# Weaving GLA blocks over the retention's projections, one pipe for both, and w_out gated page by page into DRAM

## The chip, the cores and the metric

The kernel runs on one core of one Trainium2 chip. The metric is the device time of one execution in microseconds: the median of the runs. TensorE multiplies matrices, VectorE and GpSimd work elementwise, ScalarE evaluates functions and copies, SyncE (SP) issues most DMAs. "PSUM" is TensorE's output memory, "SBUF" the memory beside it.

## The reference

Two transformer blocks follow each other on x of 1024 x 1024 (float32). The change concerns the first block's token mixer:

```python
proj = u @ w_in                                   # rq rk rv rg gq gk gv gg glr
ro = head_norm(retention(rope(rq), rope(rk), rv), center=True) * silu(rg)
log_a = log_sigmoid(glr @ gla_gate_w + gla_gate_b) / 16
go = head_norm(gla(gq / 8, gk, gv, log_a), center=False) * silu(gg)
m = concat([ro, go]) @ w_out
x = layer_norm(ALPHA * x + gate1 * m)
```

Retention and gated linear attention (GLA) have four heads each and carry a state from one stretch of the sequence to the next. `gate1` is a vector over the 1024 output columns, so `gate1 * (y @ w_out)` is `y @ (w_out * gate1)`: the kernel multiplies it into w_out's columns. The feed-forward layer, and the whole second block, follow.

## The kernel before

Every large product is made exact to about float32 by splitting each operand into a high and a low part (`split`, L82 the copy on ScalarE, L83 the subtraction on VectorE) and running three matmuls for each 128 rows of the contraction (`mm3`, L114 to L116). One output tile of 128 x 512 over a contraction of 1024 is a *group* of 24 matmuls. Weights come in pages of 128 x 1024: loaded into a page of tag S (six buffers) by SP, then split into two pages of tag W or X (eight buffers each). Pages of tag H (eight buffers) hold the blocks' data.

The order of the first mixer is written in `build` with Python generators. `gla_proj` computes GLA's projections and stores them in DRAM (g_qkb, gv, gg). Then `ret_proj` runs 24 groups, yielding after each: eight for the retention's gate (`tok_proj`, stored as rg through SP) and sixteen for its q and k (stored as r_qk through ScalarE's queue). `weave(main, side, n)` takes n steps of the side generator for each step of the main one and then runs what is left of the side.

The side is `pipe` over eight `gla_block`s of 128 tokens. One step of `pipe` starts a new block and advances each live one by a stage, the newest first. A GLA block has three stages:

- Stage 0: loads gv, gg and g_qkb (L520, L521, L523). For each of two pairs of heads, GpSimd makes seven differences (L531), ScalarE takes the absolute value and the exponential (L533, L534), VectorE multiplies q in (L536) and GpSimd k (L537). TensorE computes the scores (L544) into PSUM of tag "sc", of which there are two buffers. VectorE evicts each with a product (L549) or masked copies (L552), four evictions a buffer.
- Stage 1: decayed q and k (L560 to L564), the output matmuls (L567, L569), a transpose (L573), the state's update (L578, L583) and the statistics of the head norm (L454 and on).
- Stage 2: the gate on GpSimd (L475), transposes (L478), the scaling on ScalarE (L446), the store to g_od (L588).

The weave is 0.3: a pipe step after each 3.33 groups. When the groups are done, the rest of the GLA pipe runs. Then `ret_setup` loads tables and the weight of v (`r_W`, in W pages). `gate1` is broadcast over the partitions into a page of tag "bc" (three buffers, L73), and `wout_load` takes w_out's rows of k = 4 to 7 (four pages: load L668, gating on GpSimd L672, split into X pages). Then the pipe over eight `ret_block`s: loads of r_qk (L623 to L625), k_rot (L626) and rg (L628), the value group, the rotation (L631 on GpSimd, L632 and L633 on VectorE), scores (L637), transposes (L642), output and state (L648 to L654), head norm, store to r_od (L657). `block1_out` loads and gates the other half of w_out, into W pages that the value weight leaves, and multiplies.

The code's order is not each engine's order. The framework plans, when the program is built, the order of every engine's and every queue's instructions, with the code's order as priority and its own estimates of the durations; on the chip each engine then keeps that order and waits where something is not ready. In the trace the first gating operations of w_out stand among the GLA blocks, and the broadcast of gate1 was issued at 310.51 us, long before the code's place for it.

```python
run(n.weave(n.ret_proj(T), n.pipe(n.gla_block(i) for i in range(NB)), 0.3))
n.ret_setup()
n.gate1 = n.bcast(n.mod["gate1"][0])
n.wout = n.wout_load(I["w_out"], n.gate1, (4, 6))
run(n.pipe(n.ret_block(i, T) for i in range(NB)))
```

Of the kernel before, what the change touches and what calls it, by code (L numbers as in the profile page):

```python
# [10 lines left out]
ALU = mybir.AluOpType  # L11
# [3 lines left out]
S = 1024  # L15
D = 1024
FF = 4096
NB = 8
# [6 lines left out]
class Net:  # L25
# [21 lines left out]

    BUFS = dict(U=4, X=8, H=8, W=8, S=6, half=6, ev=4, bc=3)

# [34 lines left out]

    def wpage(self, src, r0, c0, C, kt=None, gate=None, tag="W"):
        kt = kt or 1024 // C
        st = self.page("S")
        hi = self.page(tag, F32R)
        lo = self.page(tag, F32R)
        sv = st[:, 0:kt * C]  # L90
        self.nc.sync.dma_start(
            out=sv.rearrange("p (k c) -> p k c", c=C),
            in_=src[r0:r0 + 128 * kt, c0:c0 + C].rearrange("(k p) c -> p k c", p=128))
        if gate is not None:
            self.nc.gpsimd.tensor_tensor(out=sv, in0=sv, in1=gate, op=ALU.mult)
        self.split(sv, hi[:, 0:kt * C], lo[:, 0:kt * C], self.w_eng)
        return (hi[:, 0:kt * C].rearrange("p (k c) -> p k c", c=C),
                lo[:, 0:kt * C].rearrange("p (k c) -> p k c", c=C))

    def wcols(self, src, c0, C, K=1024, tags="W"):  # L100

        per = min(1024 // C, K // 128)
        out = []
        for k in range(0, K // 128, per):
            h, l = self.wpage(src, 128 * k, c0, C, per, tag=tags[k * len(tags) // (K // 128)])
            out += [(h[:, j, :], l[:, j, :]) for j in range(per)]
        return out
# [257 lines left out]
def _rows(ap, t):  # L365
    return ap[t * 128:(t + 1) * 128, :]


class Mix1(Net):


    def feat_out(self, T, W, m, h, ps_tag="mm"):

        ps = self.ps(ps_tag)
        self.mm3(ps, [(a[:, m], b[:, m]) for a, b in W], self.act_rhs(T, h))
        return ps

    def tok_out(self, T, W, t, C=512, ps_tag="mm"):
        ps = self.ps(ps_tag)
        self.mm3(ps[:, 0:C], self.act_lhs(T, t), W)  # L380
        return ps
# [98 lines left out]

    def pipe(self, gens, oldest=False):

        live, gens, d = [], list(gens), 1 if oldest else -1
        while gens or live:
            if gens:
                live.append(gens.pop(0))
            live = [g for g in live[::d] if next(g, self) is not self][::d]
            yield

# [166 lines left out]
        yield from self.head_norm(o[:, 0], vg[:, 512:1024], self.norm_w[:, 0:4], True, A, kT)  # L656
        nc.sync.dma_start(out=self.r_od[:, :, sl], in_=kT)  # L657

    def wout_load(self, src, gate=None, ks=(0, 2, 4, 6), out=None):

        nc = self.nc
        out = out or [[None] * 8 for _ in range(2)]
        for n in range(2):
            for k in ks:
                st = self.page("S")
                tag = "W" if k < 4 else "X"
                hi, lo = self.page(tag, F32R), self.page(tag, F32R)
                nc.sync.dma_start(out=st.rearrange("p (k c) -> p k c", c=512),  # L668
                                  in_=src[128 * k:128 * k + 256, 512 * n:512 * n + 512].rearrange("(k p) c -> p k c", p=128))
                if gate is not None:  # L670
                    sv = st.rearrange("p (k c) -> p k c", c=512)
                    nc.gpsimd.tensor_tensor(out=sv, in0=sv, op=ALU.mult, in1=gate[:, 512 * n:512 * n + 512].unsqueeze(1)  # L672
                                            .broadcast_to([128, 2, 512]))
                self.split(st, hi, lo)
                for j in range(2):
                    out[n][k + j] = (hi[:, j * 512:j * 512 + 512], lo[:, j * 512:j * 512 + 512])
        return out
# [25 lines left out]
    def block1_out(self):  # L703

        nc, I = self.nc, self.I
        T = self.new_T()
        lw, lb = self.bcast(I["ln1_w"][0]), self.bcast(I["ln1_b"][0])
        self.x1d = self.dram([S, D], "x1")

        def finish(i, y):  # L710
            self.normalize(y, y, True)
            nc.vector.tensor_tensor(out=y, in0=y, in1=lw, op=ALU.mult)
            nc.vector.tensor_tensor(out=y, in0=y, in1=lb, op=ALU.add)
            nc.sync.dma_start(out=_rows(self.x1d, i), in_=y)
            self.normalize(y, y, True)
            self.to_T(y, i, T, self.mod["scale2"], self.mod["shift2"])

        W = self.wout_load(I["w_out"], self.gate1, (0, 2), self.wout)
        yield from self.out_stage(W, [(self.r_od, 4), (self.g_od, 4)], I["x"], finish)
        return T  # L720

# [1107 lines left out]
def build(tc, I, out):  # L1829
    from contextlib import ExitStack  # L1830
    with ExitStack() as ctx:
        n = Mix2(tc, ctx, I, out)
        n.modulation()
        n.kv_mem()
        def run(g):
            while True:
                try:
                    next(g)
                except StopIteration as e:
                    return e.value  # L1840

        def delay(g, k):
            for _ in range(k):
                yield
            yield from g

        norm, kv = n.first_norm(I["x"]), n.kv_proj()
        T, steps = None, [3, 0, 1, 0, 1]
        while T is None:
            n.w_eng = n.nc.gpsimd  # L1850
            for _ in range(steps.pop(0) if steps else 1):
                next(kv, None)
            n.w_eng = n.nc.vector
            T = next(norm)
        run(kv)
        def early():
            for _ in range(3):
                yield
            yield from n.mods()
            yield from n.s5_setup()  # L1860
        run(n.weave(n.gla_proj(T), early(), 0.75))
        n.gla_setup()
        run(n.weave(n.ret_proj(T), n.pipe(n.gla_block(i) for i in range(NB)), 0.3))
        n.ret_setup()
        n.gate1 = n.bcast(n.mod["gate1"][0])
        n.wout = n.wout_load(I["w_out"], n.gate1, (4, 6))
        run(n.pipe(n.ret_block(i, T) for i in range(NB)))
        T = run(n.block1_out())
        T = n.block1_mlp(T)
        n.dt_proj(T)  # L1870
        xbc = n.xbc_proj(T)
        for g, side in ((n.s5_mixer(T), (3, 1)), (n.rg_mixer(T), (1, 3))):
            for _ in g:
                for _ in range(side[0] if side else 0):
                    next(xbc, None)
                side = side[1:]
        run(xbc)
        n.ssd_setup()
        n.wout = n.wout_load(I["w_out_2"])
        out = n.block2_out()  # L1880
        T = next(out)
        run(n.weave(n.pipe(n.ssd_block(i) for i in range(NB)), delay(out, 3)))
        T = run(n.attention(T))
        n.block2_mlp(T)
# [86 lines left out]
```

## Time and profile before

| what | value |
|---|---|
| median of 3 runs | 2657.97 us (2657.94 to 2659.93) |
| the profiled execution | 2657.86 us |
| its span | 2655.9 us |
| mean granted clock of TensorE | 0.979 |
| TensorE busy | 2541.6 us, 96% |
| VectorE, ScalarE, GpSimd busy | 1879.1, 1172.0, 239.3 us |

The span is the time between the first and the last instruction of the program in the profiled execution. A clock of 1.00 is full speed, 0.50 the lower of the two levels. In rows of the timeline a bracket gives the idle time of the engine before the instruction and what ended it; "SPq" is a DMA issue on SP's queue. Times within the trace are microseconds from the span's start.

### The profile page before, as it was taken

What the parts mean: (1) busy time and instruction counts of PE and PEld (TensorE: products, weight loads), DVE (VectorE), ACT (ScalarE), POOL (GpSimd) and SP (SyncE); (2) the same over time, 40 slices, a digit from 0 to 9 for tenths busy, and PEclk for the clock granted to TensorE, in tenths of its full rate; (3) what the DMA queues carried; (4) which work ended last, traced back from release to release, by engine and by line L of the source; (5) the groups of instructions that cost most, each with busy time, mean ns of one, the idle gap of its engine ahead of it and who ended that gap; (6) DMA issues with size and microseconds to landing.
All of it is one profiled execution on the core that took longest, in us unless ns stands there. A gap on an engine that the chain in (4) does not pass through costs nothing. (4 is left out here: it accounts for less than half of the span.)

```text
span 2655.9 us, 33016 instructions
## 1 busy us (share of the span) xinstructions
PE 2541.6 (96%) x12086; PEld 2065.0 (78%) x12086; DVE 1879.1 (71%) x3205; ACT 1172.0 (44%) x1866; POOL 239.3 (9%) x222
## 2 busy tenths in 40 slices
PE   7899999889999999999999998999998999999997
PEld 6586777677888888888877776778876888888886
DVE  4858666678897777646865567785568777767786
ACT  3622233344654444433643474552237454444342
POOL 4121135540000000000000003100000000000000
PEclk8899999999999999999999999999998999999999
DMA  9772433464266569866632243361102755799783
GB/s 334 253 256 100 146 100 99 140 168 149 78 230 222 195 231 328 305 192 229 199 149 64 82 143 115 116 222 56 40 32 88 256 191 210 245 341 337 263 284 106
DMA packets 255130, 484.36 MB, mean 182 GB/s; under 512 B 21604, under 2 KB 110964, under 8 KB 254968
## 3 DMA queue, kind: packets, MB, share of 16 engines
q1 hardware_dynamic: 247768, 470.59, 52.2%
q10 hardware_dynamic: 7200, 11.67, 1.2%
q8 instruction: 95, 1.56, 0.3%
q14 instruction: 67, 0.55, 0.1%
HBM read 338.80 MB, written 143.38 MB: 182 GB/s over the span
## 5 line engine op out<-in xcount | busy, mean ns | idle before, releaser
L114 PE MATMUL ps<-U,W 128*128 128x512 f32 (+1 forms) x1080 | 427.3, 396 | 10.4 <-ACT ev L776 5.1
L115 PE MATMUL ps<-U,W 128*128 128x512 f32 (+1 forms) x1080 | 425.6, 394 | 1.5 <-DVE U L341 1.5
L114 PE MATMUL ps<-W,H 128*128 128x512 f32 x1088 | 424.4, 390 | 0.4 <-DVE X L1069 0.3
L116 PE MATMUL ps<-U,W 128*128 128x512 f32 (+1 forms) x1080 | 423.5, 392 | 0.8 <-DVE W L83 0.8
L83 DVE TENSOR_TENSOR W<-S,W 128x1024 fp32r<-128x1024 f32 (+1 forms) x272 | 333.1, 1228 | 128.5 <-ACT W L82 127.5
L115 PE MATMUL ps<-W,H 128*128 128x512 f32 x1088 | 423.9, 390 | 0.0
L116 PE MATMUL ps<-W,H 128*128 128x512 f32 x1088 | 423.9, 390 | 0.0
L82 ACT CAST W<-S 128x1024 fp32r<-128x1024 f32 x288 | 298.6, 1043 | 242.2 <-PE ps L115 161.1
L82 ACT CAST H<-S 128x1024 fp32r<-128x1024 f32 x130 | 136.6, 1050 | 287.4 <-PE ps L115 200.7
L83 DVE TENSOR_TENSOR H<-S,H 128x1024 fp32r<-128x1024 f32 x130 | 158.6, 1220 | 146.0 <-ACT H L82 141.2
L114 PEld LDWEIGHTS ps<-U,W 128*128 128x128 f32 (+1 forms) x1080 | 201.2, 186 | 60.9 <-ACT ev L776 5.4
L115 PEld LDWEIGHTS ps<-U,W 128*128 128x128 f32 (+1 forms) x1080 | 201.2, 186 | 49.5 <-DVE U L341 4.6
L114 PEld LDWEIGHTS ps<-W,H 128*128 128x128 f32 x1088 | 204.3, 188 | 43.4 <-DVE X L1069 1.2
L116 PEld LDWEIGHTS ps<-U,W 128*128 128x128 f32 (+1 forms) x1080 | 201.2, 186 | 46.8 <-DVE W L83 1.9
L116 PEld LDWEIGHTS ps<-W,H 128*128 128x128 f32 x1088 | 204.3, 188 | 41.9
L115 PEld LDWEIGHTS ps<-W,H 128*128 128x128 f32 x1088 | 204.3, 188 | 41.7
L116 PE MATMUL ps<-W,U 128*128 128x512 f32 x352 | 139.8, 397 | 5.5 <-DVE U L83 5.5
L114 PE MATMUL ps<-W,U 128*128 128x512 f32 x352 | 141.8, 403 | 2.6 <-DVE X L274 2.0
L115 PE MATMUL ps<-W,U 128*128 128x512 f32 x352 | 140.3, 398 | 0.0
L776 ACT ACTIVATE ev<-ev 128x512 f32<-128x512 f32 x104 | 65.5, 630 | 152.4 <-DVE ev L874 122.5
L116 PEld LDWEIGHTS ps<-W,U 128*128 128x128 f32 x352 | 67.0, 190 | 20.7 <-DVE U L83 6.8
L777 ACT ACTIVATE X<-ev 128x512 f32<-128x512 f32 x128 | 81.0, 634 | 3.5
(529 smaller groups left out, 4505.1 us busy)
## 6 DMA issues: line engine op xcount, KB each, us to landing
S<-mlp_h SPq DMA_DIRECT2D x112, 512.0 KB, 5.1
S<-in_w_ff SPq DMA_DIRECT2D x96, 512.0 KB, 5.1
mlp_h<-X SPq DMA_DIRECT2D x96, 512.0 KB, 4.2
S<-in_mlp_w SPq DMA_DIRECT2D x96, 512.0 KB, 4.9
mlp_w<-S SPq DMA_DIRECT2D x96, 256.0 KB, 2.5
S<-mlp_w SPq DMA_DIRECT2D x48, 512.0 KB, 4.8
S<-in_w_in SPq DMA_DIRECT2D x46, 512.0 KB, 5.3
X<-in_w_ada SPq DMA_DIRECT2D x32, 512.0 KB, 6.8
```

What stands on the lines that cost most here:

```text
L82: self.nc.scalar.copy(out=hi, in_=src)
L83: (lo_eng or self.nc.vector).tensor_tensor(out=lo, in0=src, in1=hi.bitcast(F32), op=ALU.subtract)
L114: mm(out=ps, lhsT=lh, rhs=rh, start=start and k == 0, stop=False)
L115: mm(out=ps, lhsT=lh, rhs=rl, start=False, stop=False)
L116: mm(out=ps, lhsT=ll, rhs=rh, start=False, stop=stop and k == n - 1)
L776: nc.scalar.activation(out=r, in_=x, func=ACTF.Relu)
L777: nc.scalar.activation(out=out, in_=r, func=ACTF.Square)
```

## The change

- `pipe` takes its blocks from an iterator that it asks once a step, so that the iterator can do work of its own between blocks.
- The weave is 0.42 instead of 0.3.
- `blocks()` yields the eight GLA blocks; behind each it takes one step of `gated`. Then it runs what is left of the projections, sets the retention up, yields an empty generator, and yields the eight retention blocks, with `wout_load` of k = 4 to 7 in front of the second.
- `gated` loads a page of w_out, multiplies it by gate1 on GpSimd and stores it in a DRAM tensor, one page a step, eight in all. gate1's broadcast is emitted before the projections.
- `wout_load` has no gating left; its two calls for the first mixer read the gated tensor.

```diff
     def pipe(self, gens, oldest=False):
-        live, gens, d = [], list(gens), 1 if oldest else -1
-        while gens or live:
-            if gens:
-                live.append(gens.pop(0))
+        live, gens, d = [], iter(gens), 1 if oldest else -1
+        while True:
+            g = next(gens, None)
+            if g is not None:
+                live.append(g)
+            elif not live:
+                return
             live = [g for g in live[::d] if next(g, self) is not self][::d]
             yield
...
+    def gated(self, src, gate):
+        nc = self.nc
+        d = self.dram([D, D], "gated")
+        for k in (4, 6, 0, 2):
+            for n in range(2):
+                st = self.page("S").rearrange("p (k c) -> p k c", c=512)
+                io = lambda w: w[128 * k:128 * k + 256, 512 * n:512 * n + 512].rearrange("(k p) c -> p k c", p=128)
+                nc.sync.dma_start(out=st, in_=io(src))
+                nc.gpsimd.tensor_tensor(out=st, in0=st, op=ALU.mult, in1=gate[:, 512 * n:512 * n + 512].unsqueeze(1)
+                                        .broadcast_to([128, 2, 512]))
+                nc.sync.dma_start(out=io(d), in_=st)
+                yield d
...
-    def wout_load(self, src, gate=None, ks=(0, 2, 4, 6), out=None):
+    def wout_load(self, src, ks=(0, 2, 4, 6), out=None):
...
-                if gate is not None:
-                    sv = st.rearrange("p (k c) -> p k c", c=512)
-                    nc.gpsimd.tensor_tensor(out=sv, in0=sv, op=ALU.mult, in1=gate[:, 512 * n:512 * n + 512].unsqueeze(1)
-                                            .broadcast_to([128, 2, 512]))
                 self.split(st, hi, lo)
...
-        W = self.wout_load(I["w_out"], self.gate1, (0, 2), self.wout)
+        W = self.wout_load(self.wg, (0, 2), self.wout)
...
-        run(n.weave(n.ret_proj(T), n.pipe(n.gla_block(i) for i in range(NB)), 0.3))
-        n.ret_setup()
-        n.gate1 = n.bcast(n.mod["gate1"][0])
-        n.wout = n.wout_load(I["w_out"], n.gate1, (4, 6))
-        run(n.pipe(n.ret_block(i, T) for i in range(NB)))
+        gated = n.gated(I["w_out"], n.bcast(n.mod["gate1"][0]))
+        proj = n.ret_proj(T)
+
+        def blocks():
+            for i in range(NB):
+                yield n.gla_block(i)
+                n.wg = next(gated)
+            run(proj)
+            n.ret_setup()
+            yield iter(())
+            for i in range(NB):
+                if i == 1:
+                    n.wout = n.wout_load(n.wg, (4, 6))
+                yield n.ret_block(i, T)
+
+        run(n.weave(proj, n.pipe(blocks()), 0.42))
```

## Rows read from the trace of the kernel before

**Rows 1.** The page: its first line and TensorE's busy time.
```profile
span 2655.9 us, 33016 instructions
...
PE 2541.6 (96%) x12086; PEld 2065.0 (78%) x12086; DVE 1879.1 (71%) x3205; ACT 1172.0 (44%) x1866; POOL 239.3 (9%) x222
```

**Rows 2.** Busy time by stage: stretch, length, engines, granted clock, DMA share, GB/s.
```profile
280.00:301.57 21.57, 21.57 (x96) 17.57 (x95) 16.77 (x49) 2.77 (x5) 0.00 (x0) 1.00 0.33 123
301.57:477.07 175.50, 159.13 (x965) 131.10 (x964) 102.26 (x244) 58.30 (x108) 76.01 (x108) 0.96 0.33 110
477.07:525.92 48.85, 37.06 (x257) 29.25 (x257) 39.27 (x110) 18.10 (x43) 26.36 (x13) 0.93 0.50 149
525.92:616.61 90.69, 80.27 (x490) 69.54 (x489) 69.95 (x201) 42.10 (x112) 35.59 (x22) 0.96 0.65 173
```

**Rows 3.** TensorE's waits, 301.57 to 477.07: total us, times, longest us.
```profile
PE ps L544 <- DVE half L552: 16.2, 10, 4.0
```

**Rows 4.** Timeline of TensorE: start, us, instructions, idle before and its end.
```profile
358.14 1.73 PE L544 MATMUL ps<-X,X 64*128 64x128 f32 x28
...
361.02 0.49 PE L544 MATMUL ps<-H 64*128 64x128 f32 x4 [0.55 <-DVE half L552]
...
362.99 1.16 PE L544 MATMUL ps<-X,X 64*128 64x128 f32 x16 [0.81 <-DVE half L552]
...
390.38 0.80 PE L544 MATMUL ps<-H 64*128 64x128 f32 x4 [4.00 <-DVE half L552]
390.93 3.50 PE L544 MATMUL ps<-X,X 64*128 64x128 f32 x28
...
486.40 0.80 PE L544 MATMUL ps<-H 64*128 64x128 f32 x4 [6.74 <-DVE half L552]
...
525.92 0.83 PE L637 MATMUL ps<-H 128*128 128x128 f32 x6
```

**Rows 5.** Timeline of VectorE (DVE) in a good step, a bad one, the tail.
```profile
355.20 2.05 DVE L536 TENSOR_TENSOR X<-X,H 128x896 f32<-128x896 f32 x1 [1.12 <-ACT X L534]
...
384.26 1.09 DVE L536 TENSOR_TENSOR X<-X,H 128x896 f32<-128x896 f32 x1 [8.67 <-ACT X L534]
386.46 2.00 DVE L536 TENSOR_TENSOR X<-X,H 128x896 f32<-128x896 f32 x1 [1.11 <-ACT X L534]
388.38 0.41 DVE L549 TENSOR_TENSOR half<-ps,ident 128x256 f32<-128x256 f32 x1
...
480.27 4.22 DVE L83 TENSOR_TENSOR W<-S,W 128x1024 fp32r<-128x1024 f32 x2
```

**Rows 6.** Timeline of SP's DMA issues: GLA loads and the first retention load.
```profile
374.54 0.55 SPq L523 DMA_DIRECT2D H<-g_qkb  x1
...
403.39 0.53 SPq L523 DMA_DIRECT2D H<-g_qkb  x1
...
501.77 0.53 SPq L623 DMA_DIRECT2D H<-r_qk  x1
```

**Rows 7.** Timeline of GpSimd (POOL).
```profile
379.29 5.10 POOL L531 TENSOR_TENSOR X<-H 128x128 f32<-128x128 f32 x14 [4.78 <-DMA H<-g_qkb]
385.43 2.08 POOL L537 TENSOR_TENSOR X<-X,H 128x896 f32<-128x896 f32 x1 [1.04 <-DVE X L536]
...
417.65 3.20 POOL L672 TENSOR_TENSOR S<-S,bc 128x1024 f32<-128x1024 f32 x1
```

**Rows 8.** DMA issues, 280 to 640: count, KB each, median us to landing.
```profile
r_qk<-ev ACTq DMA_DIRECT2D x16, 256.0 KB, 2.6
S<-in_w_out SPq DMA_DIRECT2D x8, 512.0 KB, 3.3
H<-r_qk SPq DMA_DIRECT2D x8, 512.0 KB, 4.7
```

**Rows 9.** A group and a line: L631 in the retention; L83 from 480 to 616.
```profile
L631 POOL TENSOR_TENSOR H<-H,half 128x1024 f32<-128x1024 f32 x6 | 14.3, 2382 | 9.9 <-DMA H<-r_qk 6.4 <-issue 3.5
...
L83 DVE TENSOR_TENSOR X<-S,X x4: 1189/1284/1789, 487.2 to 512.1; 128x1024 fp32r<-128x1024 f32 x4
```

## The prediction

> **What bounds the kernel now.** I read the page first. One core; the span is 2655.9 us and TensorE is busy for 2541.6 of it [rows 1]. The profiled execution took 2657.86 us, so 1.96 us lie around the span, and it stands 0.11 below the median of 2657.97; the sum below is made against 2657.86. About 0.2%, 5.3 us, is what a measurement of this kernel can tell from no change.
>
> Then the busy time by stage [rows 2], cut where the order of work changes: at 301.57 the first GLA scores start, at 477.07 the last of the 24 projection groups ends, at 525.92 the first retention scores start, at 616.61 the last retention block's own work on TensorE is done. What comes later the change does not touch. In the 175.50 us of the weave TensorE is busy 159.13, so 16.4 are idle. In the next 48.85, which hold the last two GLA blocks and the start of the retention, it is busy 37.06, so 11.8 are idle. In the retention's 90.69 it is busy 80.27. The change can win in the first two stretches and can lose in all three.
>
> The waits of the weave say who ends the idle time: TensorE's score matmuls (L544) wait for VectorE's masked copies (L552), ten times, 16.2 us of the 16.4 [rows 3]. TensorE waits for PSUM that VectorE frees, and the question is why VectorE is late. TensorE's timeline [rows 4] shows two kinds of steps. In a good one the scores wait 0.55 and 0.81 us, 1.4 together: by the code eight evictions must be done before the two score buffers have turned over. In a bad one they wait 4.00, and then the clock is at the lower of its two levels for a while: 28 matmuls take 3.50 instead of 1.73, the four in front 0.80 instead of 0.49. That is 4.00 + 1.77 + 0.31 = 6.1 us. Behind the first block, whose waits I put at 3.9 (VectorE is then busy with the S5 setup; 16.4 less what the other steps show), the weave has three good steps and two bad ones.
>
> VectorE's timeline gives the cause [rows 5]. In the good step the products for the next block (L536) end at 357.25, when its scores' turn has not come. In the bad one the second L536 starts at 386.46, ends at 388.46 and stands in VectorE's order in front of the first eviction (L549, 388.38) of the block whose scores are already waiting. It is late because its block's load was issued only at 374.54 [rows 6] and GpSimd's differences began at 379.29 and took 5.10 [rows 7]: 13.9 us from issue to the end of L536. Where four groups lie between two blocks this chain fits; where three lie, mostly not. The seventh block's wait of 6.74 before 486.40 [rows 4] is of the same kind, with two W splits of 4.22 in front of L549 [rows 5].
>
> **The change, part by part.** (1) Weave 0.42 for 0.3. A pipe step now comes after groups 3, 5, 8, 10, 12, 15, 17, 20 and 22; before, blocks came after groups 4, 7, 11, 14, 17, 21 and 24 (a group is 24 matmuls, and 96 take 21.57 us [rows 2], so 5.4 each). All eight blocks now score before the last groups. No arithmetic goes away: time can only come out of idle and slow-clock time.
>
> (2) One pipe. At the ninth step the rest of the projections is emitted, then the retention's setup; the second half of block 7 and the end of block 6 come behind the last group, beside the first retention blocks. What goes is a tail in which two GLA blocks have hardly a group to lie beside. It loses 11.8 us idle and some 2 by the slow clock (estimated from the granted 0.93 [rows 2]).
>
> Loss before, 301.57 to 525.92: 16.4 + 2 x 2.1 (slow clock of two bad steps) + 11.8 + 2 = 34.4 us.
>
> Loss after: the first block keeps 3.9. The seven steps behind it cost 1.4 or 6.1 each. Two or three groups lie between blocks, not three or four, so a chain of 13.9 us has less time. But each engine's order is fixed at build time by estimated times: where the scores come early enough, their evictions are placed ahead of the next block's L536, which then has a whole step. Which order each step gets is not shown. All good is 9.8, all bad 42.7. I take two bad ones, as before, since the four steps with only two groups are those whose order should flip: 5 x 1.4 + 2 x 6.1 = 19.2.
>
> The new tail: the first retention scores need group 23, the last one over the first half of the rows. A store of 2.6 and a load of 4.7 [rows 8] and a GpSimd product of 2.4 [rows 9] are 9.7, with a copy before and an add behind. Group 24, the second half of block 7 and the value matmuls of the first retention blocks lie beside it. I charge 2 us; the ends are 0 and 11.8, the old tail's idle.
>
> (3) Gating. Eight gating operations stay eight. In the trace they already stand inside late GLA steps (the first at 417.65, 3.20 us [rows 7]). Now one stands in each step, ahead of a block's differences. GpSimd is busy 76 of 175.5 us [rows 2], so this is hidden unless it falls in front of a late L531, and then it makes a bad step. Ends 0 and 8 x 3.2 = 26; I take 0.
>
> (4) DRAM. Eight stores and eight reloads of 512 KB are new, 16 issues on SP's queue. A load of w_out lands in 3.3 us [rows 8] and the DMA engines are busy a third of the weave [rows 2], which hides the transfers. The wait is the danger: SP holds each store until GpSimd has gated the page, and behind it stand the loads of gv, gg and g_qkb for a later block and the projection's weights. If that cover is gone, the late load is again a bad step. I take 0.
>
> (5) Half of w_out is now split behind the first retention block; before, four such splits of 1.28 on VectorE lay at 487 to 512 [rows 9], inside the tail. VectorE is busy 69.95 of 90.69 in the retention [rows 2], so the 5.1 us cost 0 to 5.1; I take 1, because TensorE has value matmuls to fill with. The gate's broadcast is emitted earlier, but its page comes free behind the S5 setup either way: 0.
>
> Sum: 3.9 + 19.2 + 2 + 1 = 26.1 us of loss against 34.4: 8.3 less, 2649.6, so 2650.
>
> **Rivals.** *All steps good.* Every L549 goes ahead of the next L536. Loss 3.9 + 9.8 + 2 + 1 = 16.7, time 2640. For it: three such steps exist, and GpSimd is idle most of the time. Against: both bad steps lay behind only three groups, and now never more than three lie between blocks.
>
> *The chain bounds the weave (slower).* L536 stays ahead of L549 everywhere. From one g_qkb issue to the next it is 28.9 us (374.54 to 403.39 [rows 6]), while TensorE's work for a step is now 21.5: 2.4 groups of 5.4, and 8.5 for a block (159.1 less 20 groups, by six blocks). Seven bad steps lose 42.7, all together 49.6, time 2673. It decides from four bad steps on: 3.9 + 3 x 1.4 + 4 x 6.1 + 3 = 35.5, above 34.4. For it: a load waits for an SBUF page of an earlier block, and the new stores stand on the same queue. Against: with the order flipped a block has a whole step of slack.
>
> *The tail moves but stays.* The first retention load was issued at 501.77 [rows 6], 24.7 us behind the last group, while GLA blocks still held pages of its tag H. If they do so now, the tail keeps 11.8 instead of 2: 2649.6 + 9.8 = 2659, no change.
>
> *GpSimd blocks VectorE.* The second L536 runs beside a GpSimd product (385.43 to 387.51 [rows 7]) and takes 2.00 where the first took 1.09 [rows 5]. If each of eight gating operations, now next to every block's L536, holds one by 0.9 or by its whole 3.2, that is 7 to 26 us on top: 2657 to 2676, middle 2666. The Trainium skill, page SBUF — State Buffer, section SBUF: two separate sides, says that the two engines lock a port pair for a whole instruction and the loser blocks fully. By that rule the trace agrees: L536 ends 0.95 us behind the GpSimd product, as if it had only then begun.
>
> **How the numbers follow.** Forecast (one to three bad steps) 0.45; all good 0.15; chain 0.22; tail stays 0.12; GpSimd blocks 0.06. Faster by over 0.2%: all good and 0.40 of the forecast, 0.55. Within 0.2%: three bad steps (0.05) and the tail that stays, 0.17. Slower: 0.28. The forecast's own range is 2645 to 2654. The range goes down past all good by 6 for the tail's terms, to 2634, and up to all bad, 2673.
>
> **What would show it.** In the changed profile: blocks scoring after groups 3 to 20; at most three waits of over 3 us of L544 on L552; the first L637 some 8 us before 525.9; a gating operation between all blocks. The prediction is wrong if such waits come at most steps, if L637 waits long for H<-r_qk, or if TensorE loses time behind 616 us.

## The result, and the profile after

The change makes the kernel slower. Five runs give a median of 2676.09 us (2675.12 to 2681.84) against 2657.94; the ratio is 1.0073, 95% interval 1.0058 to 1.0087, so some 19 us. The profiled execution took 2677.23 us. The page's first line and TensorE's busy time, as [rows 1]:

```profile
span 2675.5 us, 33042 instructions
...
PE 2548.2 (95%) x12086; PEld 2068.9 (77%) x12086; DVE 1881.8 (70%) x3205; ACT 1173.2 (44%) x1866; POOL 239.4 (9%) x222
```

These engines' instructions are as many as before. TensorE is busy 6.6 us longer and the span is 19.6 longer.

The busy time by stage, cut at the same events as [rows 2]: the first GLA scores start at 295.80, the last projection group ends at 527.86, the first retention scores start at 536.70. The last row goes up to the first transposes of the next stage (L182), at 655.46.

```profile
280.00:295.80 15.80, 15.80 (x71) 12.77 (x69) 11.30 (x29) 1.81 (x4) 0.00 (x0) 1.00 0.40 151
295.80:527.86 232.06, 191.06 (x1160) 155.31 (x1160) 140.23 (x349) 72.26 (x140) 95.75 (x118) 0.90 0.42 138
527.86:536.70 8.84, 8.84 (x48) 7.14 (x47) 7.10 (x19) 2.86 (x7) 2.37 (x1) 1.00 0.95 239
280.00:655.46 375.46, 321.18 (x1877) 265.60 (x1875) 241.56 (x636) 125.97 (x274) 138.46 (x143) 0.93 0.50 152
```

The same stretch before, to the same transposes:

```profile
280.00:634.22 354.22, 315.64 (x1878) 261.58 (x1877) 240.79 (x636) 125.95 (x274) 137.96 (x143) 0.96 0.45 138
```

The stretch is 21.2 us longer, and the difference of the spans (19.6) is all there. TensorE is idle 54.3 us of it where it was 38.6, so 15.7 more; the other 5.5 are busy time, with a mean granted clock of 0.93 for 0.96. Up to the first retention scores the idle time went from 28.2 (16.4 + 11.8, [rows 2]) to 41.0 (the second row: 232.06 less 191.06); behind them from 10.4 to 13.3. The old tail is gone: from the last group to the first retention scores TensorE is busy for all of the 8.84 us. The loss is inside the weave.

TensorE's waits there, as [rows 3]:

```profile
PE ps L547 <- DVE half L555: 27.9, 9, 6.7
PE ps L581 <- ACT H L578: 7.2, 2, 5.9
PE ps L114 <- ACT W L82: 4.3, 1, 4.3
```

And where they lie, in TensorE's timeline, as [rows 4] (lines are three further down: L547 are the scores, L555 the masked copies):

```profile
352.31 0.79 PE L114 MATMUL ps<-U,W 128*128 128x512 f32 x1 [4.29 <-ACT W L82]
354.59 0.80 PE L116 MATMUL ps<-U,W 128*128 128x512 f32 x1 [1.07 <-DVE W L83]
356.74 1.22 PE L581 MATMUL ps<-H,H 128*128 128x256 f32 x2 [1.35 <-ACT H L578]
364.35 0.80 PE L547 MATMUL ps<-H 64*128 64x128 f32 x4 [5.96 <-DVE half L555]
...
390.66 0.80 PE L547 MATMUL ps<-H 64*128 64x128 f32 x4 [6.71 <-DVE half L555]
...
417.05 0.80 PE L547 MATMUL ps<-H 64*128 64x128 f32 x4 [4.79 <-DVE half L555]
...
445.00 0.49 PE L547 MATMUL ps<-H 64*128 64x128 f32 x4 [0.91 <-DVE half L555]
...
471.28 1.22 PE L581 MATMUL ps<-H,H 128*128 128x256 f32 x2 [5.88 <-ACT H L578]
```

Bad steps follow each other: 12.7 us in the third step (its first four rows), then 6.71, 4.79 and 5.88; only the steps at 445 and 500 are good. The second step's 2.50 and 0.83, at 322 and 324, come before these rows. A wait costs twice: the four matmuls behind it take 0.80 us, at the lower clock, where the good step's take 0.49.

What TensorE waits for at 390.66 is in VectorE's timeline (L539 is the product with q):

```profile
387.32 1.42 DVE L539 TENSOR_TENSOR X<-X,H 128x896 f32<-128x896 f32 x1 [9.27 <-ACT X L537]
388.66 0.41 DVE L552 TENSOR_TENSOR half<-ps,ident 128x256 f32<-128x256 f32 x1
```

The next block's product still stands in front of this block's first eviction, and VectorE was idle for 9.27 us until its input came, while scores from 381.29 lay in PSUM. The order did not flip.

Why the bad steps follow each other is in two queues. First, in SP's timeline, the issues of g_qkb:

```profile
377.27 0.55 SPq L526 DMA_DIRECT2D H<-g_qkb  x1
...
403.49 0.53 SPq L526 DMA_DIRECT2D H<-g_qkb  x1
...
430.32 0.53 SPq L526 DMA_DIRECT2D H<-g_qkb  x1
...
458.54 0.53 SPq L526 DMA_DIRECT2D H<-g_qkb  x1
```

And in GpSimd's timeline L567, the product that makes the decayed k and is the last to read a block's q, k, b:

```profile
376.51 0.73 POOL L567 TENSOR_TENSOR H<-H,H 128x256 f32<-128x256 f32 x1
...
402.73 0.74 POOL L567 TENSOR_TENSOR H<-H,H 128x256 f32<-128x256 f32 x1 [8.72 <-ACT H L565]
407.09 6.96 POOL L534 TENSOR_TENSOR X<-H 128x128 f32<-128x128 f32 x14 [1.00 <-DMA H<-g_qkb]
...
429.56 0.74 POOL L567 TENSOR_TENSOR H<-H,H 128x256 f32<-128x256 f32 x1 [9.36 <-ACT H L565]
...
457.78 0.73 POOL L567 TENSOR_TENSOR H<-H,H 128x256 f32<-128x256 f32 x1
```

Each L567 ends 0.02 to 0.03 us before a load is issued (402.73 + 0.74 = 403.47, then 403.49). A new block's q, k, b wait for an H page that an earlier block gives back only in its stage 1, behind its own scores. Two such pages are in turn: the load at 403.49 is that of the sixth block, and the L567 at 402.73 that of the fourth, which scored from 381.29 on. This closes a loop: a block's load, its product in VectorE's order, behind it the evictions of the block before, that block's L567, the load after next. A turn took 26.2, 26.8 and 28.2 us. TensorE's work for a step was put at 21.5. Part of the turn looks like order alone: L567 waited for ScalarE's L565 (8.72 and 9.36 us in the rows), and L565, at 401.96, for a product of two columns of b on VectorE (L562, 401.76), whose place there is behind the statistics of a head norm (L454 to L461). Moving it was not tried.

The third step has a second cause besides: without the pages (e1, below) it still waits 6.1 us (0.66 and 5.47), with them 12.7. GpSimd's timeline there, with the gating (L671):

```profile
316.14 7.86 POOL L671 TENSOR_TENSOR S<-S,bc 128x1024 f32<-128x1024 f32 x3 [0.23 <-DMA bc<-gate]
...
337.97 2.40 POOL L671 TENSOR_TENSOR S<-S,bc 128x1024 f32<-128x1024 f32 x1 [9.61 <-DMA S<-in_w_out]
340.32 0.74 POOL L567 TENSOR_TENSOR H<-H,H 128x256 f32<-128x256 f32 x1
...
345.24 5.10 POOL L534 TENSOR_TENSOR X<-H 128x128 f32<-128x128 f32 x14 [2.92 <-DMA H<-g_qkb]
```

And SP's, with the stores of gated pages (L673), the projection's weights (L91) and a page of w_out (L670):

```profile
318.56 3.53 SPq L673 DMA_DIRECT2D gated<-S  x2
...
324.03 4.72 SPq L673 DMA_DIRECT2D gated<-S  x2
328.84 1.51 SPq L91 DMA_DIRECT2D S<-in_w_in  x2
330.44 0.61 SPq L670 DMA_DIRECT2D S<-in_w_out  x1
...
341.09 0.53 SPq L526 DMA_DIRECT2D H<-g_qkb  x1
```

The gating does not stand one page a step. All eight operations (L671) begin between 316.1 and 374.2, in the first three steps. Four pages' loads were issued by 278, and the pages sat in four of the six S buffers until the gate's broadcast had come (GpSimd's first L671, 316.14) and their stores were issued (318.56 to 328). Only then could the projection's next weights (L91) and the fifth page (L670) be loaded. GpSimd's order has the fifth page's product ahead of L567: it waited 9.61 us for that load, L567 followed at 340.32, and g_qkb at 341.09.

### The profile page after: what moved, and what is told of

It is laid out like the page before. It is cut to its first block, busy times and chain, and to the rows that moved or that the text cites. A ratio compares the mean times of both kernels' runs of the same rounds, so it can differ in the third digit from the quotient of the medians.

```text
span 2675.5 us, 33042 instructions
## 1 busy us (share of the span) xinstructions
PE 2548.2 (95%) x12086; PEld 2068.9 (77%) x12086; DVE 1881.8 (70%) x3205; ACT 1173.2 (44%) x1866; POOL 239.4 (9%) x222
## 4 chain that ended last, share of the span: by engine, by line
PE 65%; DVE 6%; ACT 3%; issue 1%; DMA 1%; SPq 0%; DVEq 0%; ACTq 0%
PE ps L116 21%; PE ps L114 21%; PE ps L115 21%; PE ps L182 1%; ACT half L186 1%; DVE st L155 1%; DVE bc L1229 0%; DVE U L83 0%; PE ps L1684 0%; DVE X L1091 0%; DVE X L1092 0%; DMA S<-v 0%; ACT H L171 0%; PE ps L1718 0%; PE ps L1784 0%
## 5 line engine op out<-in xcount | busy, mean ns | idle before, releaser
L83 DVE TENSOR_TENSOR W<-S,W 128x1024 fp32r<-128x1024 f32 (+1 forms) x272 | 337.2, 1243 | 153.9 <-ACT W L82 153.0
L114 PE MATMUL ps<-U,W 128*128 128x512 f32 (+1 forms) x1080 | 428.4, 397 | 14.6 <-ACT W L82 6.4
L114 PE MATMUL ps<-W,H 128*128 128x512 f32 x1088 | 424.4, 390 | 0.4 <-DVE X L1082 0.3
L83 DVE TENSOR_TENSOR H<-S,H 128x1024 fp32r<-128x1024 f32 x130 | 159.8, 1229 | 141.6 <-ACT H L82 136.2
L114 PEld LDWEIGHTS ps<-U,W 128*128 128x128 f32 (+1 forms) x1080 | 201.3, 187 | 64.7 <-ACT W L82 7.9
L114 PEld LDWEIGHTS ps<-W,H 128*128 128x128 f32 x1088 | 204.3, 188 | 43.4 <-DVE X L1082 1.2
L114 PE MATMUL ps<-W,U 128*128 128x512 f32 x352 | 141.0, 401 | 1.2 <-DVE X L274 0.8
```

The costliest lines, as they stand in the source:

```text
L83: (lo_eng or self.nc.vector).tensor_tensor(out=lo, in0=src, in1=hi.bitcast(F32), op=ALU.subtract)
L114: mm(out=ps, lhsT=lh, rhs=rh, start=start and k == 0, stop=False)
```

## The experiments

The differences in microseconds below are the ratio less one, times some 2657 us. "Stretch" is the length from 280.00 to the first L182 in the profile: 354.2 before, 375.5 after.

**Density or pipe?** Three kernels leave parts of the change out, a fourth goes the other way. Without the pages but with the rest (e1), and the same at 0.3 (e5):

```diff
-                nc.sync.dma_start(out=io(d), in_=st)      # gated(), all of it
+        n.wout_load(I["w_out"], n.gate1, ...)             # gating back in wout_load
# e5, besides:
-        run(n.weave(proj, n.pipe(blocks()), 0.42))
+        run(n.weave(proj, n.pipe(blocks()), 0.3))
```

> The changed kernel with the gating put back into the load of w_out (weave 0.42 and one pipe kept). Theory G: the gated pages, standing in GpSimd's and SP's orders ahead of the GLA blocks' work, cost the time; without them the waits of TensorE in the weave fall from about 41 us to about 20 and the kernel takes 2645 to 2655, below the kernel before. Theory D: the denser blocks alone miss the chain; the waits stay near 35 us or more and it takes 2668 to 2678.

> One pipe alone: the kernel before with only the common pipe (weave 0.3, w_out gated in its load). Against the run with pages at 0.3 it shows what the pages cost. Theory P (pages hold SP's, GpSimd's and tag S's places): the time is that of the kernel before or below, 2645 to 2660, so that the pages cost 14 us or more. Theory Q (the common pipe itself disturbs the order): 2668 to 2676.

The kernel before with the density alone, up and down (e3, e12):

```diff
-        run(n.weave(n.ret_proj(T), n.pipe(n.gla_block(i) for i in range(NB)), 0.3))
+        run(n.weave(n.ret_proj(T), n.pipe(n.gla_block(i) for i in range(NB)), 0.42))   # e12: 0.25
```

> The kernel before with the weave at 0.42 alone, so that all eight GLA blocks score beside the projections and the tail holds only their ends, with no pages in DRAM and no common pipe. Theory G: the tail's loss goes and nothing holds the chain, 2645 to 2655. Theory D: five or six late steps, 2668 to 2678.

> The kernel before with the weave's share 0.25 instead of 0.3, the opposite direction of the change. If the density sets how many steps wait for their block's chain, the long waits inside the weave fall from three to one or none (up to 12 us) and the uncovered tail grows by about one more block (10 to 12 us): 2653 to 2664. If the waits stay as they are, only the tail counts: 2665 to 2675.

Measured: e1 2667.84, ratio 1.0043 (1.0030 to 1.0055), 11 us; e5 2661.32, 1.0012 (1.0001 to 1.0023), 3 us; e3 2668.49, 1.0047 (1.0029 to 1.0065), 12 us; e12 2666.57, 1.0027 (1.0010 to 1.0043), 7 us. The density alone costs what e1 costs; the single pipe adds nothing at 0.42 and gains nothing at 0.3. At 0.25 the weave's long waits are gone, as the theory of the density has it:

```profile
PE ps L544 <- DVE half L552: 13.2, 13, 3.4
```

There the loads were issued every 32.4 us (347.91, 380.25, 412.67, 445.09), which is about what four groups and a block take TensorE by the prediction's figures (4 x 5.4 + 8.5 = 30.1) with 2 us of waits: the weave sets the pace, not the loop. More of the blocks are left for the tail, and the 7 us are lost there: up to 477 TensorE has got through more matmuls than before (1108 for 1058), from then to 620 through fewer (703 for 760). In e3 the issues came 25.1 to 28.1 us apart (366.39, 391.48, 418.27, 446.35), as in the changed kernel and without a page of it.

The changed kernel at 0.3 (e2) shows that the pages cost by themselves:

```diff
-        run(n.weave(proj, n.pipe(blocks()), 0.42))
+        run(n.weave(proj, n.pipe(blocks()), 0.3))
```

> The changed kernel with the weave at 0.3 again (paged gating and one pipe kept). Theory G: still slow, the pages stand in the same place, 2668 to 2678. Theory D: the chain fits again in most steps and the tail is partly closed by the pipe, 2645 to 2658.

2673.96, ratio 1.0065 (1.0045 to 1.0084): 14 us over e5, which has the same density and no pages.

**What the loop consists of.** The first theories were C, that the block's chain through GpSimd sets the step, and V, that VectorE's own load or order does. Two edits put the product with q on GpSimd (e6 in e1, e7 in the kernel before), two take the product with k off it (e9 in the kernel before, e10 in e1):

```diff
-            nc.vector.tensor_tensor(out=qt, in0=E, in1=q.unsqueeze(1)...   # e6, e7
+            nc.gpsimd.tensor_tensor(out=qt, in0=E, in1=q.unsqueeze(1)...
-            nc.gpsimd.tensor_tensor(out=E, in0=E, in1=k.unsqueeze(1)...    # e9, e10
+            nc.vector.tensor_tensor(out=E, in0=E, in1=k.unsqueeze(1)...
```

> Weave 0.42 and one pipe, no pages, and the product of E with q moved from VectorE to GpSimd, so that no late product of the next block can stand in VectorE's order in front of the evictions of this one. Theory V (that order is what makes TensorE wait at 0.42): the waits of the scores fall from about 25 us to about 12 and it takes 2645 to 2658. Theory C (the chain through the load and GpSimd itself is too long for the denser steps): GpSimd's chain is now longer, the scores wait for it, 2668 to 2685.

> The kernel before with the same move of the q product to GpSimd. Theory V: its waits of 4.00, 3.42 and 6.74 us fall to 1.4 or so, 10 to 15 us faster, 2642 to 2648. Theory C: no change or slower, 2656 to 2670.

> The kernel before with one operation moved: the product of E with k (L537, twice a block) on VectorE instead of GpSimd. In the trace of before it takes 2.08 to 3.03 us there and the product L536 of the same size 1.09 to 2.19 us on VectorE. Theory C (a step is as long as a block's chain from the decays to the scores, which goes through GpSimd): the chain loses about 2 us twice a block, the three long waits of before shrink, 2640 to 2652. Theory V (VectorE's own load or order is what a block waits for): about 2.4 us a block more on VectorE, 2658 to 2670.

> e1_no_paged_gating (blocks woven at 0.42, one pipe, no pages) with the product of E with k on VectorE. Theory C: five long waits fall by some 2 to 4 us each, 2645 to 2658. Theory V: as e1_no_paged_gating or slower, 2667 to 2680. If C holds and this comes out at or under e9_before_k_on_vector, the denser weave pays once the chain is short.

Measured: e6 2693.52, 1.0127 (1.0112 to 1.0142); e7 2677.58, 1.0065 (1.0048 to 1.0082); e9 2657.83, 0.9995 (0.9986 to 1.0005); e10 2671.04, 1.0049 (1.0033 to 1.0066). What V forecast fails with the first pair: less work on VectorE made both kernels slower, by 22 and 17 us. But the edit also puts two products of 2.1 us a block more on GpSimd, in the same loop (the loads in e6 came 26.9 to 32.4 us apart), so VectorE's order by itself is not tested by it. C in its simple form falls with the second: less work on GpSimd gained nothing, at either density. What takes one engine's 2 us off puts 1 to 2 on another that the same block needs.

**The loop's return path.** What closes the loop is a page. Two edits at once take the load out of it: the block's q, k, b go to a page of tag X, and its store goes to ScalarE's queue (e13 in the kernel before, e14 in e1, e17 in the changed kernel, e18 is e14 at 0.36):

```diff
-        qkb = self.page("H")[:, 0:768].rearrange("p (s j c) -> p s j c", s=3, c=128)
+        qkb = self.page("X")[:, 0:768].rearrange("p (s j c) -> p s j c", s=3, c=128)
...
-        nc.sync.dma_start(out=self.g_od[:, :, sl], in_=f)
+        nc.scalar.dma_start(out=self.g_od[:, :, sl], in_=f)
```

> The kernel before with a block's g_qkb loaded into a page of tag X instead of H, and the block's store (L588) issued on ScalarE's queue instead of SP's. Theory P (the block's chain is closed by the H pages and by SP's order: the loads of the next block wait for an earlier block's store): g_qkb lands well before GpSimd needs it, the waits of 3.4, 4.0 and 6.7 us fall under 2, 2643 to 2652. Theory W (the chain is the work between load and scores, in the engines' order): the loads land earlier, the long waits stay, 2655 to 2662.

> e1_no_paged_gating (0.42, one pipe, no pages) with the same two edits. Theory P: five long waits vanish, 2640 to 2652, the gain that the prediction looked for. Theory W: 2664 to 2670.

> The changed kernel with g_qkb in a page of tag X and the store L591 on ScalarE's queue. If the two causes add up (the H pages' cycle 10 us, as e14 against e1; the gating pages 4 to 8 us), 2662 to 2667. If the pages of the gating hold the loads up in another way (SP's order, the staging buffers), 2670 to 2677.

> e14_nopages_early_loads at 0.36 instead of 0.42. With the chain shorter, the waits of the weave stay at 1 to 3 us at either density and the end of the weave moves some 5 us later: 2655 to 2662, no change from e14. If the waits are still set by the density, they shrink and the time falls: 2648 to 2655, under the kernel before.

Measured: e13 2669.39, 1.0029 (1.0017 to 1.0041); e14 2657.86, 0.9993 (0.9982 to 1.0004); e17 2663.57, 1.0011 (1.0002 to 1.0021); e18 2660.55, 0.9998 (0.9988 to 1.0008).

At 0.42 the edits take back all of the density's loss (e14 against e1: 0.9993 and 1.0043, some 13 us) and in the changed kernel most of the whole (1.0011 against 1.0073, some 16 us). SP's issues in e14 come 19.9, 22.8 and 26.5 us apart:

```profile
356.74 0.53 SPq L526 DMA_DIRECT2D X<-g_qkb  x1
...
376.66 0.52 SPq L526 DMA_DIRECT2D X<-g_qkb  x1
...
399.47 0.52 SPq L526 DMA_DIRECT2D X<-g_qkb  x1
...
425.96 0.52 SPq L526 DMA_DIRECT2D X<-g_qkb  x1
```

GpSimd's differences (L534) in e14 wait for score matmuls to free their pages, hardly for the load. The load still waits for a page, now one of tag X that score matmuls (L547) free, but it comes earlier. What ended their idle time (us, times) in e14:

```profile
  PE ps L547: 24.7, 5
  DMA X<-g_qkb: 2.3, 1
```

And in e1:

```profile
  DMA H<-g_qkb: 4.4, 4
  PE ps L547: 1.7, 1
```

TensorE's waits in the weave of e14, and its stretch:

```profile
PE ps L547 <- DVE half L555: 16.1, 12, 4.1
PE ps L570 <- DVE half L555: 9.2, 5, 3.9
PE ps L547 <- ACT H L472: 2.4, 1, 2.4
```

```profile
280.00:637.97 357.97, 314.39 (x1877) 261.27 (x1877) 247.31 (x640) 129.07 (x277) 141.74 (x151) 0.97 0.45 136
```

The same two views of e1:

```profile
PE ps L547 <- DVE half L555: 25.2, 11, 5.5
PE ps L581 <- ACT H L578: 8.3, 2, 7.7
```

```profile
280.00:647.28 367.28, 318.07 (x1879) 264.16 (x1877) 239.22 (x636) 126.03 (x274) 137.42 (x143) 0.94 0.44 133
```

The sum of the waits falls little, 33.5 to 27.7, but no single wait is over 4.1 us any more, and the clock of the stretch goes from 0.94 to 0.97. Of the 9.3 us that the stretch is shorter, 5.6 are idle time and 3.7 busy time. (The two spans differ by 14.1 us; the other 5 lie behind the stretch, and e1's was the slowest of its six runs.) But the expected 2640 to 2652 did not come: waits of 1 to 4 us for VectorE's copies stay in every step. e13, where the loop was long enough already, missed on the wrong side of both its theories: behind the first block no wait of the weave was over 1.5 us up to 413 us, and waits of 3.0 to 4.3 us came between 419 and 518 for VectorE's copies and GpSimd's L564. Up to 477 it had got about as far as the kernel before (186 matmuls of L114 for 191, 418 of the scores for 377), at a granted clock of 1.00 for 0.97; from then to 620 it got through fewer, 694 for 760. So the loss lies behind the weave; why is open. Page and queue were not tried apart, and each edit also lets the framework plan all the orders anew; that the page carries the gain rests on the issues and waits shown here. No density beat the kernel before: e18 is within its 0.2%.

**What the pages cost.** e15 leaves out their product, e16 their store, e11 puts the product on VectorE; e4 loads each page a step ahead, e8 starts the pages with the fifth block, two a step:

```diff
# e15
-                nc.gpsimd.tensor_tensor(out=st, in0=st, op=ALU.mult, in1=gate...
# e16
-                nc.sync.dma_start(out=io(d), in_=st)
-                yield d
+                yield src
# e11
-                nc.gpsimd.tensor_tensor(out=st, in0=st, op=ALU.mult, in1=gate...
+                nc.vector.tensor_tensor(out=st, in0=st, op=ALU.mult, in1=gate...
# e4
+                st, io = nxt
+                if p < 7:
+                    nxt = load(*order[p + 1])
# e8
-                n.wg = next(gated)
+                for _ in range(2 if i >= 4 else 0):
+                    n.wg = next(gated)
```

> The changed kernel with each page of w_out loaded one step before it is gated, so that GpSimd does not wait for its load. Theory G, with the late load as the cause: the 9.6 and 9.0 us that GpSimd waited for S<-in_w_out go, g_qkb is loaded some 7 us earlier in the third step, and the kernel gains 8 to 15 us, 2661 to 2668. If the stores on SP's queue hold the chain instead, or theory D is right: within 4 us of 2676.

> The changed kernel with the pages gated from the fifth GLA block on, two a step, instead of one from the first. Theory P, with S pages held as the cause (four pages of w_out wait in tag S from about 230 us until the gate's broadcast lands at 316, and the q and k weights come 50 us later than before): the weights are loaded early again, TensorE's wait for a W split at 352 goes, and it takes about what the kernel without pages takes, 2664 to 2670. If stores and gating themselves cost, wherever they stand: 2672 to 2680.

> The changed kernel with the gating of the pages (L671, eight operations) on VectorE instead of GpSimd. The 8 us between it and e1_no_paged_gating lie, by one reading, in GpSimd's queue and in the port it shares with VectorE (a block's decays wait behind a page, the weights' splits take 2.2 instead of 1.2 us): then 2667 to 2671. By the other they lie in the staging buffers that the pages hold and in the DMA issues: then 2673 to 2679, as the changed kernel.

> The changed kernel without the product of the pages with the gate: the pages are loaded, stored to DRAM and loaded again, and w_out goes in without its gate (the output leaves it out). If the 8 us over e1_no_paged_gating lie in GpSimd's time, 2666 to 2670 (pages go through without waiting for the gate's broadcast either); if in the transfers, 2673 to 2679.

> The changed kernel with the product of the pages kept and its store left out: w_out is then read from its input, without the gate (the output leaves it out). If the 8 us lie in GpSimd's time or in the staging buffers held until the broadcast, 2673 to 2679; if in the stores and the second reading, 2666 to 2670.

Measured: e4 2674.53, 1.0073 (1.0054 to 1.0091); e8 2675.29, 1.0059 (1.0042 to 1.0075); e11 2672.00, 1.0051 (1.0034 to 1.0068); e15 2671.42, 1.0041 (1.0027 to 1.0055); e16 2671.02, 1.0036 (1.0023 to 1.0049). e15 and e16 are both back at e1's 1.0043, though each takes away only half of what a page does; so in these two orders neither GpSimd's time nor the transfers cost by themselves. What both shorten is the stay in the S buffers: without the product a page goes out as soon as it has landed, without the store its buffer is free as soon as it is gated (still only behind the broadcast; the first L91 of the third step in e16 is issued at 319.91, against 328.84). In e16 the load that the changed kernel issues at 341.09 is on its way 7 us earlier:

```profile
334.20 0.53 SPq L526 DMA_DIRECT2D H<-g_qkb  x1
```

e4 missed. GpSimd's wait for its pages fell from 18.6 to 1.8 us and g_qkb was issued at 337.42, but the next page's product now stood ahead of the differences:

```profile
341.86 2.41 POOL L679 TENSOR_TENSOR S<-S,bc 128x1024 f32<-128x1024 f32 x1 [1.83 <-DMA S<-in_w_out]
344.46 5.10 POOL L534 TENSOR_TENSOR X<-H 128x128 f32<-128x128 f32 x14 [0.20 <-DMA H<-g_qkb]
```

They began at 344.46, against 345.24 in the changed kernel and 337.29 in e1: two products in a row can hold the same loop. e8 did not do what it set out to: emitted from the fifth block on, the gating still stood at 317.3 to 381.7 us, since each page's operations need nothing that comes late and the plan draws them forward. Yet only two pages waited for the broadcast there, six of the projection's weight pages were issued by 275, g_qkb at 333.97 (e1: 333.67), and TensorE's waits for W splits were gone. It is no faster than the changed kernel all the same: its third step waits 8.3 us and its fourth 8.5, where two products begun at 379.40 stand between the two halves of a block's differences. By its own expectation that speaks against the S buffers as the only cause. Shown is that the 8 us go when either the product or the store goes; by which way they come is open, and it differs with the order. e11 lies between; its interval overlaps those of e1 and of the changed kernel, so what of the loss is on GpSimd alone is not settled.

## Why the prediction was wrong

Forecast 2650 (2634 to 2673), measured 2676: wrong in sign, and outside the range.

- *What bounds it, and the two kinds of steps:* right. Most of the loss after is still waits of score and state matmuls for VectorE and ScalarE, and a step is good (1.3 and 1.7 us) or bad, with one of 3.3 between.
- *(1), the step that failed:* "I take two bad ones, as before, since the four steps with only two groups are those whose order should flip." It came out the other way round. Two groups lay in front of the second, fourth, fifth and seventh block (16 and 24 matmuls of L114 between the scores tell two groups from three), and all four of these waited: 3.3, 6.71, 4.79 and 5.88 us. Of the three with three groups two were good; the third step's 12.7 has the pages in it, and is 6.1 without them. The order did not flip, and the load was not free to come earlier, because its page came back from an earlier block's L567. The prediction names that page, and the 28.9 us between two issues of g_qkb [rows 6], only as evidence for a rival. The 28.9 alone could not decide, since e12 shows that a slow weave sets the period too. But in the trace before SP's loads already waited for GpSimd's L564, the line that L567 is now:

```profile
SPq L520 <- POOL H L564: 4.6, 3, 1.5
```

By e3 the density alone costs 12 us; e14, with page and queue changed together, takes it back, and its loads and waits point to the page.

- *(2), the tail:* it went as forecast, with no idle time between the last group and the first retention scores where 2 us were charged. What that gained does not show in the time: the single pipe at 0.3 (e5) is 3 us slower than before, within what is no change.
- *(3), gating at 0:* wrong, and so was "now one stands in each step": all eight stood in the first three. The term's ends, 0 to 26, hold the 8 us that lie between e1 and the changed kernel.
- *(4), DRAM at 0:* the transfers were hidden, as said, and the danger was named (SP and the loads behind it). That pages wait in S buffers for a broadcast, and keep the projection's weights out, was not; how much of the 8 us that is stays open (e8).
- *(5), splits behind the retention block:* the retention's stretch has 2.9 us more idle time where 1 was charged; not tried by itself.
- *Rivals:* "the chain bounds the weave" is what happened, and a chance of 0.22 was too low. That its price (2673) lies near the measured 2676 is luck: it is for seven bad steps. With five the prediction's own sum gives 3.9 + 2 x 1.4 + 5 x 6.1 + 3 = 40.2 of loss, so 2664; the kernel without pages took 2668, and the pages' 8 us came on top. The tail's rival fell. "GpSimd blocks VectorE" is part of the third step, below, but e16, with all eight products left on GpSimd, is back at e1's time and leaves it no price of its own.

## What to carry to other kernels

Before making a pipelined side job denser, follow its buffers round: from a load to what frees the buffer for the next load. If that takes longer per step than the work of a new step, the wait moves into the short steps. Here moving a product between engines did not take it out, and a page of another tag with the store on another queue did; an earlier release by order was not tried. And a "spread" of side work in the code's order is no spread on the engines: look where the plan puts it, and in which buffers it waits.

## What the runs showed of the hardware

VectorE's splits of weights took about twice as long beside products on GpSimd as without them: 1.21 us at best in this stretch, but in the changed kernel's third step

```profile
352.29 2.25 DVE L83 TENSOR_TENSOR W<-S,W 128x1024 fp32r<-128x1024 f32 x1 [0.40 <-ACT W L82]
...
360.55 2.43 DVE L83 TENSOR_TENSOR W<-S,W 128x1024 fp32r<-128x1024 f32 x1
```

The first ends at 354.54, 1.08 us behind a GpSimd product (L540) that ran from 351.36 to 353.46; the second ended as long behind one of two L671 that began at 358.58 and took 6.62 together. With the gating on VectorE (e11), three of the four splits took 1.21 to 1.39. The Trainium skill, page SBUF — State Buffer, section SBUF: two separate sides, says that an operation of VectorE with two SBUF inputs and one of GpSimd that reads SBUF take a shared port pair as an exclusive lock for a whole instruction. The trace agrees.

The load of the fifth page, issued at 330.44 among two stores and three loads of the same size, was there for GpSimd only at 337.97, 7.5 us later; the median from issue to landing before was 3.3 [rows 8].
